# Strassen's seven products for 18 of the 22 gate/up pairs of each feed-forward, in a two-layer float32 decoder

## The chip, the cores and the metric

One NeuronCore of a Trainium2 chip runs the whole program. The metric is the device time of one execution in microseconds (us), as the median over runs. The engines are TensorE (PE; its weight loads are shown apart as PEld), VectorE (DVE), ScalarE (ACT), GpSimd (POOL), and SyncE (SP), whose queue issues most transfers.

## The reference

The input is one sequence of 512 tokens with 1024 features, in float32. Layer 0 is feed-forward, short gated convolution, feed-forward; layer 1 is feed-forward, differential attention over shared keys and values, feed-forward. Each of the four feed-forwards is

```
gate, up = jnp.split(x @ w_gu, 2, axis=-1)      # x: 512 x 1024, w_gu: 1024 x 5632
return (jax.nn.silu(gate) * up) @ w_down        # w_down: 2816 x 1024
```

with a norm before and after it. The change concerns the first product, `x @ w_gu`.

## The kernel before

Everything is kept as float32 and multiplied in three parts: a matrix is split into a rounded part `hi` (type fp32r) and the rest `lo`, and a product is hi·hi + hi·lo + lo·hi. The weights' `hi` is written by ACT (line 152) and `lo` by DVE (line 153); the activations `x_hi` and `x_lo` lie in SBUF transposed, features on the partitions, in 8 blocks of 128 features (`KT`) by 512 tokens.

The 2816 gate columns and 2816 up columns are handled as 22 pairs. A pair is one transfer of 1 MB (`raw`, two buffers) and two units: 1024 x 128 gate weights and 1024 x 128 up weights. For each unit `proj` runs 8 blocks x 3 parts = 24 matmuls of 512 tokens (line 169), into one of the two banks of a PSUM tile `gu`; ACT then takes silu of the gate (line 372), and DVE multiplies it by the up part into `praw` (line 374). The first three pairs of a feed-forward that follows another stage run in halves: first tokens 0 to 255, while the last tokens are still being normalized, then tokens 256 to 511 (`by_halves`). The feed-forward of layer 1 that follows the keys and values does not do so.

`down` then multiplies by `w_down` (line 220) in an order of its own (`two_then_two`), with `praw` split into `psp` just ahead. `WBUFS = 7` split units are held ahead of their use. PSUM holds three tiles `acc` of two banks and one tile `tp`, in which transposes are put. The order of instructions on each engine comes from a scheduler; each engine runs its queue in order.

Of the kernel before, what the change touches and what calls it, by code (L numbers as in the profile page):

```python
# [9 lines left out]
F32 = mybir.dt.float32  # L10
# [8 lines left out]
P = 128  # L19
# [11 lines left out]
WBUFS = 7  # L31
# [9 lines left out]
class Ahead:  # L41
# [21 lines left out]
    def done(self, i):  # L63
        self.closed.add(i)
        self.items[i] = None
        self.pump()

# [24 lines left out]
def trunk(ctx, tc, x, gu, dn, norm_g, cin, ck, cout, kvg, wk, wv, wq, lamp, subg, wo, out):  # L92
# [19 lines left out]

    def col_pairs(ap):
        return [ap[i].rearrange("p u k c -> p u (k c)") for i in range(ap.shape[0])]
# [5 lines left out]
    pairs, base = [], {}  # L120

    def stream(key, srcs):
        base[key] = 2 * len(pairs)
        pairs.extend(srcs)

    stream("gu00", col_pairs(gu[0, 0]))
    stream("dn00", row_pairs(dn[0, 0]))
    stream("cin", col_pairs(cin))
    stream("cout", row_pairs(cout))
    stream("gu01", col_pairs(gu[0, 1]))  # L130
    stream("dn01", row_pairs(dn[0, 1]))
    stream("k", col_pairs(wk))
    stream("v", row_pairs(wv))
    stream("gu10", col_pairs(gu[1, 0]))
    stream("dn10", row_pairs(dn[1, 0]))
    stream("q", col_pairs(wq))
    stream("wo", row_pairs(wo))
    stream("gu11", col_pairs(gu[1, 1]))
    stream("dn11", row_pairs(dn[1, 1]))
# [6 lines left out]
    raws = Ahead(load_pair, 2, len(pairs))  # L146

    def split_unit(i):
        raw = raws.get(i // 2)[:, i % 2, :]
        hi = wpool.tile([P, D], F32R, tag="whi", bufs=WBUFS, name="whi")  # L150
        lo = wpool.tile([P, D], F32R, tag="wlo", bufs=WBUFS, name="wlo")
        nc.scalar.activation(hi, raw, AF.Copy)  # L152
        nc.vector.tensor_tensor(lo, raw, hi.bitcast(F32), ALU.subtract)  # L153
        if i % 2:
            raws.done(i // 2)
        return hi, lo

    weights = Ahead(split_unit, WBUFS, 2 * len(pairs))


    def proj(o, key, u, xk, cols, ks=range(KT)):

        hi, lo = weights.get(base[key] + u)
        n = cols.stop - cols.start
        for k in ks:
            c = slice(k * P, (k + 1) * P)
# [6 lines left out]
    def close(key, u):  # L173
        weights.done(base[key] + u)
# [10 lines left out]
    def down(key, seq, parts, finish, tp_token=0, bufs=3):  # L185
# [22 lines left out]
        for n, (f, t) in enumerate(seq):  # L208
            if f is None:
                finish(t, y[t])  # L210
                continue
            if t not in y:
                if t >= 2:
                    later.keep(0)
                y[t] = tp_tile("y") if t == tp_token else acc_tile("y")
            hi, lo = weights.get(base[key] + f)
            ph, pl = ring.get(item_of[n])(t)
            for a, b in ((ph, hi), (ph, lo), (pl, hi)):
                for c in range(2):
                    nc.tensor.matmul(y[t][:, c, :], a, b[:, c * 512:(c + 1) * 512],  # L220
                                     start=(f == first[t] and a is ph and b is hi),
                                     stop=(f == last[t] and a is pl))
# [119 lines left out]
    def raw_parts(pool, praws):  # L342
        def parts(f, toks):
            a, n = toks[0] * P, len(toks) * P
            ps = pool.tile([P, 2, S], F32R, tag="psp", bufs=3, name="psp")
# [9 lines left out]
    def ffn(pool, l, i, xT, finish, halves=3):  # L355
# [5 lines left out]
        def job(f):  # L361
            def go(cols):
                if f not in tiles:
                    tiles[f] = acc_tile("gu")
                ps = tiles[f]
                for s in range(2):
                    proj(ps[:, s, :], "gu" + key, 2 * f + s, xk_of(xT), cols)
                    if cols.stop == S:
                        close("gu" + key, 2 * f + s)
                if cols.stop == S:  # L370
                    sil = pool.tile([P, S], F32, tag="sil", bufs=2, name="sil")
                    nc.scalar.activation(sil, ps[:, 0, :], AF.Silu)  # L372
                    praws[f] = place(f)
                    nc.vector.tensor_tensor(praws[f], sil, ps[:, 1, :], ALU.mult)  # L374
            return go

        by_halves([job(f) for f in range(NF)], halves)
# [5 lines left out]
    def conv(pool, xT, finish):  # L383
# [6 lines left out]
        def job_cz(ch):  # L390
            def go(cols):
# [7 lines left out]
                if cols.stop == S:  # L399
                    c = pool.tile([P, S], F32, tag="sil", bufs=2, name="c")  # L400
# [57 lines left out]
    def shared_kv(pool, xkv):  # L458
        tiles = {}

        def job(hd):
            def go(cols):
# [5 lines left out]
                if cols.stop == S:  # L468
                    close("k", hd)
                    kk = pool.tile([P, 2, S], F32R, tag="psp", bufs=3, name="kk")  # L470
# [14 lines left out]
        later.keep(0)  # L485

# [6 lines left out]
        def finish(t, y):  # L493
            for n in range(2):
                vs = pool.tile([P, S], F32, tag="sil", bufs=2, name="vs")
# [217 lines left out]
    with tc.tile_pool(name="big0", bufs=1, reuse_waits="tile") as pool:  # L713
# [4 lines left out]
        ffn(pool, 1, 0, holder["xT"], next_xT(norm_g[1, 2]), halves=0)  # L718
# [62 lines left out]
```

## Time and profile before

| | |
|---|---|
| median of 3 runs (range) | 1936.1 us (1936.01 to 1938.53) |
| the profiled execution | 1934.57 us |
| its span, first to last instruction | 1932.8 us |
| mean granted TensorE clock, as a share of full speed | 0.998 |
| busy: PE / DVE / ACT / POOL | 1897.1 / 752.3 / 616.9 / 99.6 us |
| read from HBM | 187.38 MB |

A busy PE is not necessarily a PE at its peak: a matmul's record is longer than the distance to the next one, since matmuls are pipelined. The distance between starts is therefore what a matmul costs. A row of idle time names what ended it.

### The profile page before, as it was taken

The numbers are of one execution on the slowest core, as the hardware profiler recorded it, in microseconds if no ns is written. First come the engines' busy times: TensorE is split into PE (matmuls) and PEld (weight loads), VectorE is DVE, ScalarE is ACT, GpSimd is POOL, SyncE is SP. The second block draws the span as 40 slices with busy tenths as digits, with TensorE's granted clock in tenths as the row PEclk, the third lists the DMA queues.
The fourth block names the chain that finished last, engine by engine and source line by source line (L and its number), as shares of the span: only waits on it lengthen the run. The fifth ranks groups of instructions, "written<-read, shape, count | busy, mean of one in ns | idle before, by whom it ended". The sixth has DMA issues, their size and how long they took to land. (4 is left out here: it accounts for less than half of the span.)

```text
span 1932.8 us, 22286 instructions
## 1 busy us (share of the span) xinstructions
PE 1897.1 (98%) x9376; PEld 1594.7 (83%) x9376; DVE 752.3 (39%) x978; ACT 616.9 (32%) x939; POOL 99.6 (5%) x234
## 2 busy tenths in 40 slices
PE   7999999999999999999999999999999999999998
PEld 7888888898889888888988888888886798888886
DVE  4322233554463222233633222233668463222333
ACT  4222222432243222223523222222457442222222
POOL 1000000000010000000200000000113210000000
PEclk9999999999999999999999999999999999999999
DMA  5332322232323232221354222222322033222221
GB/s 211 110 109 87 109 87 95 80 131 87 109 81 116 87 109 87 103 93 65 133 176 160 87 108 89 95 102 87 131 104 88 28 113 117 87 105 92 89 86 44
DMA packets 41508, 197.20 MB, mean 102 GB/s; under 512 B 3648, under 2 KB 8000, under 8 KB 27584
## 3 DMA queue, kind: packets, MB, share of 16 engines
q1 hardware_dynamic: 39616, 189.49, 27.6%
q0 software_dynamic: 1792, 6.29, 0.8%
q8 instruction: 73, 1.20, 0.2%
q14 instruction: 27, 0.22, 0.0%
HBM read 187.38 MB, written 8.39 MB: 101 GB/s over the span
## 5 line engine op out<-in xcount | busy, mean ns | idle before, releaser
L153 DVE TENSOR_TENSOR wlo<-raw,whi 128x1024 fp32r<-128x1024 f32 x328 | 401.1, 1224 | 770.0 <-ACT whi L152 769.6
L152 ACT ACTIVATE whi<-raw 128x1024 fp32r<-128x1024 f32 x328 | 346.3, 1057 | 833.1 <-PE gu L169 682.4
L169 PE MATMUL gu<-x_hi,whi 128*128 128x512 f32 (+1 forms) x1552 | 575.1, 371 | 1.3 <-ACT x_hi L297 1.3
L169 PE MATMUL gu<-x_lo,whi 128*128 128x512 f32 (+1 forms) x1552 | 574.6, 370 | 1.1 <-DVE x_lo L298 1.1
L169 PE MATMUL gu<-x_hi,wlo 128*128 128x512 f32 (+1 forms) x1552 | 574.4, 370 | 0.0
L220 PE MATMUL y<-whi,psp 128*128 128x512 f32 x1536 | 413.4, 390 | 0.0
L220 PEld LDWEIGHTS y<-whi,psp 128*128 128x128 f32 x1536 | 287.7, 188 | 59.3
L169 PEld LDWEIGHTS gu<-x_hi,whi 128*128 128x128 f32 x1552 | 293.8, 189 | 51.2 <-ACT x_hi L297 1.7
L169 PEld LDWEIGHTS gu<-x_lo,whi 128*128 128x128 f32 x1552 | 293.8, 189 | 50.1 <-DVE x_lo L298 1.4
L169 PEld LDWEIGHTS gu<-x_hi,wlo 128*128 128x128 f32 x1552 | 293.7, 189 | 49.5
L220 PE MATMUL y<-wlo,psp 128*128 128x512 f32 x768 | 236.6, 389 | 0.0
L220 PEld LDWEIGHTS y<-wlo,psp 128*128 128x128 f32 x768 | 144.2, 188 | 30.1
L298 DVE TENSOR_TENSOR psp<-praw,psp 128x512 fp32r<-128x512 f32 (+1 forms) x126 | 70.5, 563 | 250.3 <-ACT psp L297 250.3
L297 ACT ACTIVATE psp<-praw 128x512 fp32r<-128x512 f32 (+1 forms) x126 | 66.6, 528 | 317.5 <-PE y L220 309.0
L278 POOL TENSOR_SCALAR rb<-ss 128x1 f32<-128x1 f32 x84 | 27.1, 322 | 1737.7 <-ACT junk L275 1733.4
L374 DVE TENSOR_TENSOR praw<-sil,gu 128x512 f32<-128x512 f32 x88 | 59.8, 680 | 1.4 <-ACT sil L372 1.4
L169 PE MATMUL cz<-x_hi,whi 128*128 128x512 f32 (+1 forms) x160 | 55.6, 348 | 0.0
L169 PE MATMUL cz<-x_lo,whi 128*128 128x512 f32 (+1 forms) x160 | 55.4, 347 | 0.0
L169 PE MATMUL cz<-x_hi,wlo 128*128 128x512 f32 (+1 forms) x160 | 55.4, 347 | 0.0
L372 ACT ACTIVATE sil<-gu 128x512 f32<-128x512 f32 x88 | 50.8, 577 | 0.0
L308 DVE SCALAR_TENSOR_TENSOR xn<-h,rs,gpre 128x1024 f32<-128x1024 f32 x28 | 35.8, 1283 | 36.2 <-POOL rs L280 23.8
L280 POOL TENSOR_TENSOR rs<-rb,mhalf 128x1 f32<-128x1 f32 x84 | 49.2, 586 | 7.0
(105 smaller groups left out, 1313.6 us busy)
## 6 DMA issues: line engine op xcount, KB each, us to landing
raw<-gu SPq DMA_DIRECT2D x88, 1024.0 KB, 4.7
raw<-dn SPq DMA_DIRECT2D x44, 1024.0 KB, 4.7
raw<-cin SPq DMA_DIRECT2D x12, 1024.0 KB, 4.7
raw<-cout SPq DMA_DIRECT2D x4, 1024.0 KB, 4.8
raw<-wk SPq DMA_DIRECT2D x4, 1024.0 KB, 4.8
raw<-wv SPq DMA_DIRECT2D x4, 1024.0 KB, 5.4
kscr<-kk POOLq DMA_DIRECT2D x8, 512.0 KB, 6.3
raw<-wq SPq DMA_DIRECT2D x4, 1024.0 KB, 4.9
```

The costliest lines, as they stand in the source:

```text
L152: nc.scalar.activation(hi, raw, AF.Copy)
L153: nc.vector.tensor_tensor(lo, raw, hi.bitcast(F32), ALU.subtract)
L169: nc.tensor.matmul(o[:, cols], a[:, c], b[:, cols], start=(k == 0 and b is xh and a is hi), stop=(k == KT - 1 and a is lo))
L220: nc.tensor.matmul(y[t][:, c, :], a, b[:, c * 512:(c + 1) * 512], start=(f == first[t] and a is ph and b is hi), stop=(f == last[t] and a ...
L278: nc.gpsimd.tensor_scalar(b, ss, m / n, m * EPS, ALU.mult, ALU.add)
L280: nc.gpsimd.tensor_tensor(r, b, mhalf, ALU.pow)
L297: nc.scalar.activation(hi, src, AF.Copy)
L298: nc.vector.tensor_tensor(lo, src, hi.bitcast(F32), ALU.subtract)
L308: nc.vector.scalar_tensor_tensor(xn, h[t], r, g, ALU.mult, ALU.mult)
L372: nc.scalar.activation(sil, ps[:, 0, :], AF.Silu)
L374: nc.vector.tensor_tensor(praws[f], sil, ps[:, 1, :], ALU.mult)
```

## The change

Pairs 4 to 21 of each feed-forward (72 in all) are computed by one level of Strassen's algorithm in Winograd's form. The left matrix of a pair has four quarters of 512 features x 128 columns: `a11` and `a12` are the gate weights of the first and second 512 features, `a21` and `a22` the up weights. The right matrix has four quarters of 512 features x 256 tokens. Seven products of quarters (4 blocks x 3 parts = 12 matmuls of 256 tokens each) take the place of eight.

- Left factors (`Sum`): a11, a12, a22 as they are, and s1 = a21+a22, s2 = s1-a11, s3 = a11-a21, s4 = a12-s2. DVE forms the sums in PSUM (tile `sums`, in the place of `tp`), ACT writes `hi`, and `lo` comes from DVE for sums and from POOL for plain quarters.
- Right factors (`RightFactors`), once for each feed-forward: POOL puts x together again as `xr`, DVE forms t1 to t4; t1, t2, t3 take the place of three weight tiles `wt`, and t4 overwrites a quarter of `x_hi`/`x_lo`.
- The products go into three accumulators `a`, `b`, `c` (256 columns each; pairs take turns between the two banks). Between products, partial results are read out: u1 by ACT, u2, u3, g2 and both up halves `su` by DVE; POOL does the last multiplication into `praw`.
- Weights are held in 8 half tiles `wf` (512 features, hi and lo) and 3 whole tiles `wt`, together as much as the 7 units before. Units of the other stages use both kinds by turns; in a half tile a unit takes two ACT and two DVE instructions.

```diff
+            plain = {"a11": a11, "a12": a12, "a22": a22}.get(self.form)
+            if plain is not None:
+                nc.scalar.activation(hi, plain, AF.Copy)
+                nc.gpsimd.tensor_tensor(lo, plain, hi.bitcast(F32), ALU.subtract)
+                Sum.flush()
+            else:
+                if self.form == "s2":
+                    Sum.psum = tp_tile("sums")
+                s0, s1 = Sum.psum[:, 0, :], Sum.psum[:, 1, :]
+                if self.form == "s2":
+                    nc.vector.tensor_tensor(s0, a21, a22, ALU.add)
+                    nc.vector.tensor_tensor(s1, s0, a11, ALU.subtract)
+                    src = s1
+                elif self.form == "s1":
+                    src = s0
+                elif self.form == "s3":
+                    Sum.flush()
+                    nc.vector.tensor_tensor(s0, a11, a21, ALU.subtract)
+                    src = s0
+                else:
+                    Sum.flush()
+                    nc.vector.tensor_tensor(s1, a12, s1, ALU.subtract)
+                    src = s1
+                nc.scalar.activation(hi, src, AF.Copy)
+                Sum.flush()
+                Sum.pending.append((self, lambda: nc.vector.tensor_tensor(lo, src, hi.bitcast(F32), ALU.subtract)))
...
+    FORMS = ("a11", "s2", "s1", "s3", "a12", "s4", "a22")
...
+            self.x = pool.tile([P, KT, S], F32, tag="praw", bufs=3, name="xr")
+            for k in range(0, KT, 2):
+                nc.gpsimd.tensor_tensor(self.x[:, k:k + 2, :], self.hi[:, k:k + 2, :].bitcast(F32),
+                                        self.lo[:, k:k + 2, :].bitcast(F32), ALU.add)
...
+            def after6():
+                nc.vector.tensor_tensor(u2, b, u1, ALU.add)
+
+            def after7():
+                nc.vector.tensor_tensor(u3, b, u1, ALU.add)
+                nc.vector.tensor_tensor(su[:, 1, RIGHT], c, u3, ALU.add)
+
+            def after3():
+                nc.vector.tensor_tensor(g2, c, u2, ALU.add)
+                nc.scalar.activation(su[:, 0, RIGHT], g2, AF.Silu)
+
+            def after4():
+                nc.vector.tensor_tensor(su[:, 1, LEFT], b, u1, ALU.add)
+                praws[f] = place(f)
+                nc.gpsimd.tensor_tensor(praws[f], su[:, 0, :], su[:, 1, :], ALU.mult)
+
+            step(a, "a11", "b11", True, True, lambda: nc.scalar.activation(u1, a, AF.Copy))
+            step(b, "s2", "t2", True, True, after6)
+            step(c, "s1", "t1", True, True, lambda: None)
+            step(b, "s3", "t3", False, True, after7)
+            step(a, "a12", "b21", False, True, lambda: nc.scalar.activation(su[:, 0, LEFT], a, AF.Silu))
+            step(c, "s4", "b22", False, True, after3)
+            step(b, "a22", "t4", False, True, after4)
...
+        right.four()
+        for f in range(PLAIN, NF):
+            seven(f, (f - PLAIN) % 2)
```

**DVE, in the middle of a feed-forward's gate/up stage.** Before, a pair has two `lo` parts of weights and the multiplication by silu (the numbers tell tiles apart):

```order
L153 TENSOR_TENSOR wlo_4396<-raw_4307,whi_4395 128x1024
L374 TENSOR_TENSOR praw_4092<-sil_4399,gu_4340 128x512
L153 TENSOR_TENSOR wlo_4428<-raw_4307,whi_4427 128x1024
L153 TENSOR_TENSOR wlo_4458<-raw_4369,whi_4457 128x1024
L374 TENSOR_TENSOR praw_4092<-sil_4461,gu_4402 128x512
```

Now a pair has thirteen, in this order: L598 is u2, L229 the `lo` of a sum, L221 the sum s3, L601 is u3, L602 the right half of `su` (it reads `c`), L225 the sum s4, L605 g2, L214 and L215 the sums s1 and s2 of a later pair, L609 the left half of `su`. The tile `u_775` belongs to the pair that PE multiplies; `sums_791` are the factors of the next pair, `sums_917` those of the one after it:

```order
L598 TENSOR_TENSOR u_775<-b_650,u_775 128x256
L229 TENSOR_TENSOR wf_790<-sums_791,wf_790 128x512
L229 TENSOR_TENSOR wf_808<-sums_791,wf_808 128x512
L221 TENSOR_TENSOR sums_791<-raw_639 128x512
L601 TENSOR_TENSOR u_775<-b_650,u_775 128x256
L229 TENSOR_TENSOR wf_823<-sums_791,wf_823 128x512
L602 TENSOR_TENSOR su_776<-c_651,u_775 128x256
L225 TENSOR_TENSOR sums_791<-raw_639,sums_791 128x512
L229 TENSOR_TENSOR wf_858<-sums_791,wf_858 128x512
L605 TENSOR_TENSOR u_775<-c_651,u_775 128x256
L214 TENSOR_TENSOR sums_917<-raw_756 128x512
L609 TENSOR_TENSOR su_776<-b_650,u_775 128x256
```

Between u3 (L601) and the right half of `su` (L602), which frees `c`, the `lo` part of s3 (L229) has been put; the sum for a later pair (L214) stands ahead of the left half of `su` (L609), which frees `b`.

**PE, at the same place.** Before, units follow each other in groups of three matmuls (here the last group of the gate and the first of the up unit):

```order
L169 MATMUL gu_934<-x_hi_96,whi_740 128x512
L169 MATMUL gu_934<-x_lo_97,whi_740 128x512
L169 MATMUL gu_934<-x_hi_96,wlo_741 128x512
L169 MATMUL gu_934<-x_hi_96,whi_772 128x512
L169 MATMUL gu_934<-x_lo_97,whi_772 128x512
L169 MATMUL gu_934<-x_hi_96,wlo_773 128x512
```

Now, from the end of the product with a12 (`wf_1090`) to the product with s4 (`wf_1107`); `wf_1124` is a22:

```order
L336 MATMUL a_1147<-x_lo_97,wf_1090 128x256
L336 MATMUL a_1147<-x_hi_96,wf_1090 128x256 x2
L336 MATMUL a_1147<-x_lo_97,wf_1090 128x256
L336 MATMUL a_1147<-x_hi_96,wf_1090 128x256
L336 MATMUL b_1148<-x_hi_96,wf_1124 128x256
L336 MATMUL b_1148<-x_lo_97,wf_1124 128x256
L336 MATMUL c_1149<-x_hi_96,wf_1107 128x256
L336 MATMUL c_1149<-x_lo_97,wf_1107 128x256
L336 MATMUL c_1149<-x_hi_96,wf_1107 128x256 x2
```

Two of the twelve matmuls of the product with a22 have been moved ahead of the product with s4; the other ten follow it. This is so in 17 of the 18 pairs of a feed-forward; in the last one they stand in the order of the code.

**POOL, at the same place.** Before, POOL has no instruction there. Now it has four for each pair, three `lo` parts of plain quarters (L207: a12 and a22 of the next pair, a11 of the one after) and the multiplication into `praw` (L611):

```order
L207 TENSOR_TENSOR wf_841<-raw_639,wf_841 128x512
L207 TENSOR_TENSOR wf_875<-raw_639,wf_875 128x512
L207 TENSOR_TENSOR wf_895<-raw_756,wf_895 128x512
L611 TENSOR_TENSOR praw_445<-su_776 128x512
L207 TENSOR_TENSOR wf_967<-raw_756,wf_967 128x512
```

The multiplication of a pair stands behind three splits, of which the third is for a pair two places on.

## Rows read from the trace of the kernel before

**Rows 1.** The page: busy us (share of the span) and instructions; granted clock in tenths.

```profile
PE 1897.1 (98%) x9376; PEld 1594.7 (83%) x9376; DVE 752.3 (39%) x978; ACT 616.9 (32%) x939; POOL 99.6 (5%) x234
...
PEclk9999999999999999999999999999999999999999
```

**Rows 2.** Groups by line and form: count | busy us, mean ns | idle before, releaser.

```profile
L169 PE MATMUL gu<-x_hi,whi 128*128 128x512 f32 x1264 | 491.7, 389 | 0.0
...
L153 DVE TENSOR_TENSOR wlo<-raw,whi 128x1024 fp32r<-128x1024 f32 x328 | 401.1, 1224 | 770.0 <-ACT whi L152 769.6
L152 ACT ACTIVATE whi<-raw 128x1024 fp32r<-128x1024 f32 x328 | 346.3, 1057 | 833.1 <-PE gu L169 682.4 <-PE cz L169 57.6 <-PE b L169 28.4
```

**Rows 3.** Waits of PE: us in total, times, longest.

```profile
PE xps L313 <- DVE xn L308: 12.8, 6, 9.8
...
PE gu L169 <- ACT x_hi L297: 1.3, 1, 1.3
```

**Rows 4.** PE in order of time, 256 tokens wide, first feed-forward: start us, us.

```profile
40.00 0.28 PE L169 MATMUL gu<-x_hi,wlo 128*128 128x256 f32 x1
...
42.88 0.28 PE L169 MATMUL gu<-x_hi,wlo 128*128 128x256 f32 x1
```

**Rows 5.** PE in order of time, 512 tokens wide, first feed-forward.

```profile
101.50 0.39 PE L169 MATMUL gu<-x_hi,whi 128*128 128x512 f32 x1
...
104.22 0.39 PE L169 MATMUL gu<-x_hi,whi 128*128 128x512 f32 x1
```

**Rows 6.** Groups by line and form, DVE and ACT, smaller tiles.

```profile
L298 DVE TENSOR_TENSOR psp<-praw,psp 128x512 fp32r<-128x512 f32 x66 | 45.7, 692 | 174.5 <-ACT psp L297 174.5
L298 DVE TENSOR_TENSOR psp<-praw,psp 128x256 fp32r<-128x256 f32 x60 | 24.9, 421 | 75.7 <-ACT psp L297 75.7
...
L297 ACT ACTIVATE x_hi<-att_ps 128x512 fp32r<-128x512 f32 x8 | 4.7, 593 | 7.3 <-PE att_ps L633 6.4 <-DVE m L574 0.9
```

**Rows 7.** DVE in order of time, two like instructions back to back, merged (two stretches).

```profile
366.25 0.75 DVE L298 TENSOR_TENSOR psp<-praw,psp 128x256 fp32r<-128x256 f32 x2
...
962.92 1.28 DVE L298 TENSOR_TENSOR kk<-kps,kk 128x512 fp32r<-128x512 f32 x2
```

**Rows 8.** In order of time: PE's last matmul into b, and DVE's reading of b.

```profile
437.32 0.39 PE L169 MATMUL b<-x_hi,wlo 128*128 128x512 f32 x1
...
437.75 0.69 DVE L420 TENSOR_TENSOR praw<-praw,b 128x512 f32<-128x512 f32 x1 [0.61 <-PE b L169]
```

**Rows 9.** In order of time: DVE frees a PSUM bank, and PE goes on.

```profile
970.71 0.69 DVE L298 TENSOR_TENSOR kk<-kps,kk 128x512 fp32r<-128x512 f32 x1 [0.32 <-ACT kk L297]
...
971.45 0.50 PE L169 MATMUL kps<-xkv,whi 128*128 128x256 f32 x2 [0.25 <-DVE kk L298]
...
971.79 0.28 PE L169 MATMUL kps<-xkv,wlo 128*128 128x256 f32 x1
...
971.91 0.40 PE L169 MATMUL kps<-xkv,whi 128*128 128x256 f32 x2
```

**Rows 10.** Instructions of one tile, POOL: count, duration ns min/median/max.

```profile
L537 POOL TENSOR_SCALAR bias<-dist x8: 613/617/922, 1388.4 to 1490.1; 128x512 f32<-128x512 f32 x8
...
L617 POOL TENSOR_TENSOR rr<-rs,r x32: 189/190/729, 1431.1 to 1523.6; 128x1 f32<-128x1 f32 x32
```

**Rows 11.** In order of time: a small POOL instruction under DVE's xn.

```profile
936.04 0.55 POOL L280 TENSOR_TENSOR rs<-rb,mhalf 128x1 f32<-128x1 f32 x1
...
936.62 1.28 DVE L308 SCALAR_TENSOR_TENSOR xn<-h,rs,gpre 128x1024 f32<-128x1024 f32 x1 [0.71 <-POOL rs L280]
...
936.84 1.48 POOL L280 TENSOR_TENSOR rs<-rb,mhalf 128x1 f32<-128x1 f32 x1
```

**Rows 12.** In order of time: POOL beside a DVE instruction that reads PSUM.

```profile
1388.39 1.20 POOL L537 TENSOR_SCALAR bias<-dist 128x512 f32<-128x512 f32 x2
1388.45 1.28 DVE L287 SCALAR_TENSOR_TENSOR tmp<-y,rs,gpost 128x1024 f32<-128x1024 f32 x1 [0.97 <-POOL rs L280]
```

**Rows 13.** Transfers: queue, count, KB each, us from issue to landing.

```profile
raw<-gu SPq DMA_DIRECT2D x88, 1024.0 KB, 4.7
```

More of the change, by code (lines that the diff above doesn't have):

```diff
@@ L66, in done, with __init__, free, take @@
         self.pump()
+class Slots:
+    def __init__(self, cap):
+        self.cap, self.given = cap, []
+    def free(self, n):
+        i = len(self.given) - self.cap
+        return all(self.given[j] for j in range(max(i, 0), max(i + n, 0)))
+    def take(self):
+        self.given.append(False)
+        return len(self.given) - 1
+    def give(self, i):
+        self.given[i] = True
 class Later:
@@ L144, in load_pair @@
         return raw
[L146 to L158, printed above, removed]
+    raws = Ahead(load_pair, 2)
@@ new lines, in trunk, with __init__, free, make @@
+    class Sum:
+        pending = []
+        psum = None
+        def __init__(self, pair, form):
+            self.pair, self.form = pair, form
+        def free(self):
+            return half_slots.free(1)
+        def make(self):
+            raw = raws.get(self.pair)
+            a11, a12, a21, a22 = (raw[:, u, h * 512:(h + 1) * 512] for u in range(2) for h in range(2))
+            w, slot = half_tile()
+            hi, lo = w[:, 0, :], w[:, 1, :]
+            self.halves, self.slots = [(hi, lo)], [slot]
+            plain = {"a11": a11, "a12": a12, "a22": a22}.get(self.form)
[17 more added lines that the diff above has]
+                    src = s0
+                else:
+                    Sum.flush()
[4 more added lines that the diff above has]
+                Sum.pending.append((self, lambda: nc.vector.tensor_tensor(lo, src, hi.bitcast(F32), ALU.subtract)))
+            if self.form == FORMS[-1]:
+                raws.done(self.pair)
+        @staticmethod
+        def flush():
+            while Sum.pending:
+                Sum.pending.pop(0)[1]()
+        def ready(self):
+            if any(e is self for e, _ in Sum.pending):
+                Sum.flush()
@@ new lines, in trunk, with add_units, add_sums @@
+    FORMS = ("a11", "s2", "s1", "s3", "a12", "s4", "a22")
+    def add_units(key, srcs, kind):
+        for j, src in enumerate(srcs):
+            pairs.append(src)
+            for u in range(2):
+                index[key, 2 * j + u] = len(entries)
+                entries.append(Unit(len(pairs) - 1, u, kind(2 * j + u)))
+    def add_sums(key, f, src):
+        pairs.append(src)
+        for form in FORMS:
+            index[key, f, form] = len(entries)
+            entries.append(Sum(len(pairs) - 1, form))
@@ L171, in proj, with close, product @@
             later.tick(3 * 0.21 * n / 512)
-    def close(key, u):
-        weights.done(base[key] + u)
+    def close(*key):
+        weights.done(*key)
+    def product(o, key, xk, first, last):
+        hi, lo = weights.get(*key)[0]
+        for k in range(4):
+            c = slice(k * P, (k + 1) * P)
+            xh, xl = xk(k)
+            for a, b in ((hi, xh), (hi, xl), (lo, xh)):
+                nc.tensor.matmul(o, a[:, c], b, start=(first and k == 0 and b is xh and a is hi),
+                                 stop=(last and k == 3 and a is lo), skip_group_check=True)
+            later.tick(3 * 0.21 * 256 / 512)
     def two_then_two(nf, tail, stag):
@@ new lines, in seven, with step @@
+        def seven(f, e):
+            if e == 0:
+                tiles["abc"] = [acc_tile(n) for n in "abc"]
+            a, b, c = (t[:, e, LEFT] for t in tiles["abc"])
+            tmp = work.tile([P, 4, 256], F32, tag="tmp", bufs=2, name="u")
+            u1, u2, u3, g2 = (tmp[:, n, :] for n in range(4))
+            su = pool.tile([P, 2, S], F32, tag="pair", bufs=3, name="su")
+            def step(o, form, factor, first, last, then):
+                product(o, ("gu" + key, f, form), right.t[factor], first, last)
+                then()
+                if f == NF - 1 and factor in right.slots:
+                    right.done(factor)
+                close("gu" + key, f, form)
+            def after6():
[8 more added lines that the diff above has]
+                nc.vector.tensor_tensor(su[:, 1, LEFT], b, u1, ALU.add)
+                praws[f] = place(f)
+                nc.gpsimd.tensor_tensor(praws[f], su[:, 0, :], su[:, 1, :], ALU.mult)
[6 more added lines that the diff above has]
+            step(b, "a22", "t4", False, True, after4)
@@ L378, in ffn @@
+        if halves:
+            later.keep(2)
+            for f in range(3):
+                job(f, FIRST)
+            later.keep(0)
+            right = RightFactors(pool, xT)
+        for f in range(PLAIN):
+            job(f, SECOND if halves and f < 3 else ALL)
+            if f == 1:
+                right.one_three()
+            if f == 2:
+                right.two()
+        right.four()
+        for f in range(PLAIN, NF):
+            seven(f, (f - PLAIN) % 2)
         g_post = bcast(norm_g[l, 1 if i == 0 else 5], "gpost")
```

175 lines of the change are left out of this document (129 added, 46 removed).

## The prediction

> **What bounds the kernel now.** I read the page of the profile first, then the groups by line and form, the waits of PE, and short stretches in order of time. PE is busy 98% of the span at a granted clock of 0.998 of full speed, the upper of its two levels (2.4 GHz) [rows 1]. Its longest wait totals 12.8 us, and on this stage's matmuls it waits 1.3 us once, at the start [rows 3]. So the kernel is as long as its matmuls, and a matmul costs the distance to the next start. 512 tokens wide, twelve steps take 104.22 - 101.50 = 2.72 us, 0.2267 us each, though the record says 0.39 [rows 5]. 256 wide, 24 steps take 42.88 - 40.00 = 2.88 us, 0.120 us each [rows 4]. Half the width is thus more than half the price: 0.2267 = 2 x 0.1067 + 0.0133, a fixed 0.013 us for each matmul.
>
> DVE and ACT wait for PE here: ACT's splits of weights spent 682.4 us waiting for PE to free a tile, and DVE's waited for ACT's [rows 2]. They have room; the question is whether they have enough, and in time.
>
> **PE's work.** A pair had 2 units x 24 = 48 matmuls of 512 tokens: 48 x 0.2267 = 10.88 us. It gets 7 x 12 = 84 of 256: 84 x 0.120 = 10.08 us. That is 0.80 us less, 7.4% instead of the 12.5% that seven for eight suggests, because 84 fixed parts replace 48. For 18 x 4 = 72 pairs: **-57.6 us**. Weights loaded afresh for every matmul are in the 0.120 already, since the row's kernel loads them so too.
>
> The Trainium skill, "TensorE: Matmul & The Clock Gate", section "Wait — 56ns, not 53.3ns?", gives for another number type a spacing of columns / 2.4 GHz + 2.5 ns; an estimate by it is 84 x 0.109 against 48 x 0.216 us, 1.19 us a pair, -86 us in all. The rows show a fixed part five times as large, so I go by them.
>
> **Load of the other engines in a pair.** Two DVE instructions of 512 elements back to back start 1.28 - 0.68 = 0.60 us apart, two of 256 start 0.75 - 0.42 = 0.33 us apart, each ending about 0.09 later than its successor starts [rows 6, 7]. DVE gets 4 sums and 4 lo parts of 512, and 5 results of 256: 8 x 0.60 + 5 x 0.33 = 6.5 us of 10.08. ACT gets 7 hi parts and three of 256: 7 x 0.59 + 3 x 0.42 = 5.4 us at most, the 0.42 taken from DVE [rows 6]. No row has DVE writing float32 sums to PSUM; the bounds are 0.60 us (as in every row) and 1.2 us (write as dear as read). I take 0.60, since reading PSUM makes no difference either (kk, psp).
>
> POOL gets four two-input instructions of 512 elements; no row has one. With one input 512 elements took 617 ns, and a two-input one of a single element 190 ns [rows 10], so an element costs about (617 - 190) / 512, 0.43 us for 512. Low bound 0.62 us (the second input free), high 0.19 + 4 x 0.43 = 1.9 us (four passes); I take two passes, 0.19 + 0.86 = 1.05 us, 4.2 us a pair.
> The Trainium skill, "GPSIMD Engine Reference", section 3.1, has 4497 ns for 2048 elements, from which 1.1 to 1.3 us is an estimate here.
>
> **The chain that matters.** `b` and `c` are read between two products that write them. Take the pair's first matmul as 0: products start at 0 (a11), 1.44 (s2), 2.88 (s1), 4.32 (s3), 5.76 (a12), and end at 10.08. Of a22, two matmuls run at 7.20, ahead of s4, which starts at 7.44. A reader starts 0.04 us after the record of the last matmul ends [rows 8]; the 256-wide record is 0.28 long [rows 4], so 0.20 us after the next start. PE goes on 0.05 us after DVE's record ends (970.71 + 0.69 to 971.45), and its second matmul then starts 0.22 instead of 0.12 later: 0.10 for the restart [rows 9].
>
> - u2 at 2.88 + 0.20 = 3.08; lo(s2) and lo(s1) from 3.41 to 4.61; then the sum s3, which waits for the end of lo(s1), from 4.7 to 5.4; ACT's hi(s3) to 6.05.
> - s3's product ends at 5.76, so u3 starts at 5.96, lo(s3) at 6.29 (hi is 0.24 early), the half of su that reads c at 6.89. It ends at 7.31; PE may write c at 7.36.
> - s4's product is due at 7.44. **0.08 us to spare**, less than the restart's 0.10. I charge 0.02 us a pair: 1.4 us.
>
> In the last pair of each feed-forward the two matmuls were not moved; there s4 is due at 7.20 and loses 0.16 + 0.10 us: 4 x 0.26 = 1.0 us. Behind this wait stands everything on PE, and a delay moves the whole pair. The others have more room: u2 frees b at about 3.55 for 4.32; the left su frees b at 10.08 + 0.20 + 0.42 + 0.05 = 10.75 for 11.52; u1 is needed 2.9 us after ACT can do it.
>
> **Once in each feed-forward.** POOL's four sums of 1024 elements for `xr` take about 4 x 1.9 = 7.6 us, and the t factors cost DVE 8 x 1.13 = 9 us and ACT 4 us. In three feed-forwards they lie under the second halves of pairs 0 to 2 and under pair 3 (3 x 24 x 2 x 0.120 + 10.88 = 28 us), in the other under 43 us of whole pairs. I charge 0; without the cover it would be up to 9 us each. Splitting a unit by halves costs two fixed parts (0.07 us each on DVE) in engines that wait; the ring still holds seven units' worth, and where it is refilled late, at a stage's end, the first units are split 2 us before their use. `raw` is loaded in 4.7 us [rows 13], as often as before, one in 10 us. At the kernel's start the first unit's second part may add 0.1 us.
>
> **Sum.** -57.6 + 1.4 + 1.0 + 0.1 = -55.1. The profiled execution took 1934.57 us (span 1932.8), 1.5 under the median: 1934.57 - 55.1 = 1879.5, span 1877.7, and for the median 1936.1 - 55.1 = **1881 us**. What a measurement can tell from no change is about 0.2%, 4 us.
>
> **Rivals.**
>
> *c comes late* (0.22). 0.08 us is little: dearer PSUM writes put hi(s3) behind u3 (a sum of 1.2 us ends at 5.9, hi at 6.6, su at 7.6, 0.2 late, with restart 0.3), and so does any wait of DVE between u3 and su. Against it: every duration is from a row of the same shape. 0.1 to 0.4 us a pair: 1888 to 1910 us.
>
> *POOL gets in ahead of the sum s1* (0.08). An instruction of DVE with two SBUF inputs and one of POOL shut each other out: under `xn` POOL's took 1.48 us instead of 0.55 and ended 0.42 after xn [rows 11], while beside `tmp`, whose large input is PSUM, POOL ran its usual 0.6 [rows 12]. That DVE waits in its turn, no row shows. Of a pair's DVE instructions only two sums have two SBUF inputs, s1 and s3. DVE reaches s1 of a later pair at about 9.5, POOL its split of a22 at 9.76. Were POOL first, s1 would start at 10.8, the left su at 11.4, and b be free at 11.87 instead of by 11.52; 0.35 + 0.10 us, in every second pair (the other takes another bank): 36 x 0.45 = +16, 1897 us.
> The Trainium skill, "SBUF — State Buffer", section "Who interferes with whom", states this as a rule: the shared port is a lock that goes to whoever starts first. By that rule the order at 9.5 decides, and the trace agrees for POOL's side (1.48 us).
>
> *POOL holds up s3: slower* (0.05). POOL's queue for a pair runs from the end of s1's sum, 10.2, through two splits and the multiplication, to 10.2 + 3P, which is 0.12 + 3P in the next pair, where DVE wants the sum s3 at 4.7. s3 can be 0.24 + 0.08 late; so from P = 1.63 us the chain slips, and with the restart's 0.10 a pair loses the 0.80 that it gained from P = 1.9. At 1.9, the high bound, it is 5.82 - 5.02 + 0.10 = 0.9 us, 72 x 0.9 = 65 us: 1944 us. Against it: it takes nearly twice the 1.05 that I work out.
>
> *A smaller fixed part* (0.02). If the new matmuls paid a fifth of the 0.0133 us, a pair would take 84 x (0.1067 + 0.0027) = 9.2 us, 1.7 less: 72 x 1.7 = 122, 1817 us with the same losses. Against it: the run of 256 wide matmuls, in the same three-part sequence, paid it in full [rows 4].
> This is what the spacing in "TensorE: Matmul & The Clock Gate" (the Trainium skill, the section named above) would make of the new matmuls; the rows disagree with it, at 0.120 us.
>
> *Setting up the factors shows* (0.05): up to 9 us in each feed-forward, 1881 + 36 = 1917 us.
>
> **How the numbers follow.** The forecast's case, 1877 to 1886, has 0.58. The range, 1875 to 1906, takes in most of the late c and POOL ahead of s1, about 0.85 in all. Faster by over 0.2%: 0.94; slower: 0.05, the case of POOL; within 0.2%: 0.01.
>
> **What would show it.** Right: 84 matmuls a pair 0.120 apart, pairs 10.1 us apart, PE waiting for L602 by at most some hundredths, POOL's 512 near 1.05 us, its splits of a22 behind the sum s1. Wrong: idle time of PE before c's matmuls that DVE ends, each pair (the chain); before b's in every second pair (POOL first); POOL above 1.6 us; a gap before pair 4 (factors).

## The result, and the profile after

In one comparison the changed kernel took 1909.2 us (median of 4 runs, 1908.2 to 1910.8) and the kernel before 1937.3 us: a ratio of 0.9855, 95% interval 0.9838 to 0.9872. It is faster, by half of what was forecast: 1881 us was predicted, 1906 was the upper end of the range, and the time lies 3 us above it. The profiled span fell from 1932.8 to 1907.8 us, by 25.0. The sums below go by these two profiles; by the medians the gain is 28.1 us, because the profiled run of before (1934.57 us) was faster than all four of this comparison and that of the changed kernel (1910.82 us) the slowest of its four.

The page of the kernel after (busy us, share, instructions; then groups), to be read beside [rows 1] and [rows 2]:

```profile
PE 1861.6 (98%) x11968; PEld 1677.9 (88%) x11968; DVE 1109.1 (58%) x1837; ACT 828.9 (43%) x1566; POOL 528.2 (28%) x538
...
PEclk9999999999999999999999999999999999999999
...
L207 POOL TENSOR_TENSOR wf<-raw,wf 128x512 fp32r<-128x512 f32 x216 | 294.2, 1374 | 440.3 <-ACT wf L206 440.3
```

PE is still busy for 98% of the span at the same clock, so the share says nothing of what went wrong. The two views that do are the stretches of the 18 Strassen pairs of each feed-forward (start:end, length, busy time of the product's line) and the waits (us in total, times, longest). First the stretches, from the first a11 matmul to the first matmul of the down product:

```profile
65.43:253.23 187.80, 185.71 (x1512) 182.22 (x1511) 1.00 0.31 107
607.12:794.72 187.60, 185.71 (x1512) 182.22 (x1511) 1.00 0.32 107
1059.36:1246.98 187.62, 185.72 (x1512) 182.22 (x1511) 1.00 0.32 107
1591.81:1779.41 187.60, 185.71 (x1512) 182.21 (x1511) 1.00 0.32 107
sum 750.62, PE 742.86 PEld 728.87; mean PE 185.71 PEld 182.22
```

1512 matmuls are 18 x 84, all of them. 72 pairs at 10.08 us would be 725.8 us; they took 750.6, or 10.42 us a pair. **24.9 us are lost here.** The other (57.6 - 24.9) - 25.0 = 7.7 us are lost elsewhere; by the medians it would be 4.6. The waits of the kernel after, to be read beside [rows 3]:

```profile
PEld c L336 <- DVE su L602: 21.6, 68, 0.7
...
DVE wf L229 <- POOL praw L611: 17.8, 63, 0.6
...
PE xps L477 <- DVE xn L472: 15.7, 10, 9.1
```

The weights of the matmuls that write `c` wait for line 602, the half of `su` that reads `c`: 68 times, in every pair but the last of each feed-forward. That is the rival *c comes late*. One pair in order of time, of which the first matmul stood at 127.95 (its a12 product, 5.76 later, starts at 133.71; L206 is ACT's `hi` of a plain quarter, here a12 of the next pair):

```profile
130.47 1.31 POOL L611 TENSOR_TENSOR praw<-su 128x512 f32<-128x512 f32 x1
...
131.09 0.60 ACT L227 ACTIVATE wf<-sums 128x512 fp32r<-128x512 f32 x1 [0.57 <-PE b L336]
131.10 0.42 DVE L598 TENSOR_TENSOR u<-b,u 128x256 f32<-128x256 f32 x1 [1.92 <-PE b L336]
131.79 1.29 DVE L229 TENSOR_TENSOR wf<-sums,wf 128x512 fp32r<-128x512 f32 x2 [0.26 <-POOL praw L611]
...
133.11 0.70 DVE L221 TENSOR_TENSOR sums<-raw 128x512 f32<-128x512 f32 x1
...
133.91 0.42 DVE L601 TENSOR_TENSOR u<-b,u 128x256 f32<-128x256 f32 x1
133.93 0.60 ACT L227 ACTIVATE wf<-sums 128x512 fp32r<-128x512 f32 x1 [2.24 <-PE b L336]
...
134.42 0.62 ACT L206 ACTIVATE wf<-raw 128x512 fp32r<-128x512 f32 x1
...
134.56 0.69 DVE L229 TENSOR_TENSOR wf<-sums,wf 128x512 fp32r<-128x512 f32 x1 [0.23 <-ACT wf L227]
...
135.17 0.41 DVE L602 TENSOR_TENSOR su<-c,u 128x256 f32<-128x256 f32 x1
135.27 0.28 PE L336 MATMUL b<-x_lo,wf 128*128 128x256 f32 x1
...
135.64 0.39 PE L336 MATMUL c<-x_hi,wf 128*128 128x256 f32 x1
135.86 0.28 PE L336 MATMUL c<-x_lo,wf 128*128 128x256 f32 x1
...
137.85 0.69 DVE L214 TENSOR_TENSOR sums<-raw 128x512 f32<-128x512 f32 x1
...
138.14 1.55 POOL L207 TENSOR_TENSOR wf<-raw,wf 128x512 fp32r<-128x512 f32 x1 [1.73 <-ACT wf L206]
```

`u2` (line 598) starts at 3.15 of the pair, where 3.08 was forecast. Then lo(s2) (line 229, the first of two) should follow 0.33 us behind; it follows after 0.69, at 3.84. Of the 0.43 us against the forecast's 3.41, `u2` brings 0.07 and the wait 0.36. What follows is late: the sum s3 at 5.16, hi(s3) from 5.98 to 6.58 instead of until 6.05, `u3` on time at 5.96, lo(s3) at 6.61, and `su` from 7.22 to 7.64. `c` was due 0.12 after b's second matmul, at 135.39 (7.44 of the pair); it starts at 135.64, 0.25 late, and its second matmul comes 0.22 instead of 0.12 later. That is 0.35 us in this pair; the 24.9 us over the 68 pairs that stop are 0.37 each.

The row of hi(s3) names PE's product with s3 as its releaser. That can't be: in the code the `hi` of the next pair's s3 is written when the product with s1 has released its half tile, ahead of the product with s3. It follows the sum s3 by 0.12 us here, and by 0.11 in the next kernel below, where the row names the sum.

What held lo(s2)? ACT's hi(s1) runs until 131.69, and POOL's multiplication until 131.78; DVE starts at 131.79. (hi(s1) itself starts no earlier because, by the ring of eight half tiles, it is written into the tile that the product with s2 has just released: its row names PE's `b`, as that of `u2` does.) The row of lo(s2) names POOL. Two theories: **ACT** (lo(s2) waits for hi(s1), though it doesn't use it: both read the tile `sums`) and **POOL** (its multiplication holds DVE). Before them stands the reckoning of the prediction, that it waits for neither.

### The profile page after: what moved, and what is told of

Read it like the earlier page. It is cut to its first block, busy times and chain, and to the rows that moved or that the text cites. A ratio compares the mean times of both kernels' runs of the same rounds, so it can differ in the third digit from the quotient of the medians.

```text
span 1907.8 us, 29851 instructions
## 1 busy us (share of the span) xinstructions
PE 1861.6 (98%) x11968; PEld 1677.9 (88%) x11968; DVE 1109.1 (58%) x1837; ACT 828.9 (43%) x1566; POOL 528.2 (28%) x538
## 5 line engine op out<-in xcount | busy, mean ns | idle before, releaser
L207 POOL TENSOR_TENSOR wf<-raw,wf 128x512 fp32r<-128x512 f32 x216 | 294.2, 1374 | 440.3 <-ACT wf L206 440.3
L384 PE MATMUL y<-wf,psp 128*128 128x512 f32 x1344 | 310.2, 389 | 0.0
L384 PEld LDWEIGHTS y<-wf,psp 128*128 128x128 f32 x1344 | 251.8, 188 | 51.9
L229 DVE TENSOR_TENSOR wf<-sums,wf 128x512 fp32r<-128x512 f32 x288 | 192.4, 689 | 100.5 <-ACT wf L227 82.4
L178 ACT ACTIVATE wf<-raw 128x512 fp32r<-128x512 f32 x214 | 131.1, 626 | 243.3 <-PE y L384 126.2
L336 PE MATMUL b<-wt,wf 128*128 128x256 f32 x1728 | 230.8, 283 | 0.0
L336 PE MATMUL a<-x_hi,wf 128*128 128x256 f32 x1152 | 230.8, 283 | 0.0
L384 PE MATMUL y<-wt,psp 128*128 128x512 f32 x960 | 222.6, 389 | 0.0
L336 PEld LDWEIGHTS b<-wt,wf 128*128 128x128 f32 x1728 | 217.7, 192 | 0.0
L336 PEld LDWEIGHTS a<-x_hi,wf 128*128 128x128 f32 x1152 | 190.1, 192 | 0.2
L206 ACT ACTIVATE wf<-raw 128x512 fp32r<-128x512 f32 x216 | 136.1, 630 | 69.0 <-PE c L336 37.7
```

Of the source, the lines that this page charges most:

```text
L178: nc.scalar.activation(hi, raw[:, a * 512:(a + 1) * 512], AF.Copy)
L206: nc.scalar.activation(hi, plain, AF.Copy)
L207: nc.gpsimd.tensor_tensor(lo, plain, hi.bitcast(F32), ALU.subtract)
L229: Sum.pending.append((self, lambda: nc.vector.tensor_tensor(lo, src, hi.bitcast(F32), ALU.subtract)))
L336: nc.tensor.matmul(o, a[:, c], b, start=(first and k == 0 and b is xh and a is hi), stop=(last and k == 3 and a is lo), skip_group_check=True)
L384: nc.tensor.matmul(y[t][:, c, :], a, w[c][b], start=(f == first[t] and a is ph and b == 0), stop=(f == last[t] and a is pl))
```

## The experiments

### c read first

```
+def after1():                                            # behind the product s1
+    nc.vector.tensor_tensor(u3, c, u1, ALU.add)
 def after7():
-    nc.vector.tensor_tensor(u3, b, u1, ALU.add)
-    nc.vector.tensor_tensor(su[:, 1, RIGHT], c, u3, ALU.add)
+    nc.vector.tensor_tensor(su[:, 1, RIGHT], b, u3, ALU.add)
 ...
-step(c, "s1", "t1", True, True, lambda: None)
+step(c, "s1", "t1", True, True, after1)
```

> The half of su that needs c is built the other way round: v = c + u1 as soon as s1's product is in c, then su = b + v after s3's product. As many DVE instructions of the same size; c is read 1.4 us before its next product is due, b as early as before. Both theories (the first lo part waits for ACT's hi(s1), or for POOL's multiplication) put the loss on c being read too late, so both expect the 0.25 us stall and the 0.09 us restart to vanish: pairs 10.08 us apart instead of 10.42, 72 x 0.342 = 24.6 us less, 1885 us (1882 to 1889). If pairs stay above 10.3 us apart, c's reader is not what PE waits for.

It took 1895.3 us (ratio to before 0.9791, 0.9777 to 0.9806), 10 us over what both theories gave. No matmul waits for `c` any more: all steps to it are 0.120 us. The edit also changed PE's order: the two matmuls of a22 now stand behind the product with s4 in all 72 pairs (below, b's first at 135.12 follows c's last), so `c` was due at 7.20 of the pair and not at 7.44, and was still in time. It is so in the next kernel too, and in those with POOL's split behind s1 and c read first. But another wait stands in its place, as the waits of this kernel show:

```profile
PE b L336 <- DVE su L611: 5.3, 32, 0.4
```

32 of the 72 pairs now stop before b's first product. In order of time:

```profile
135.00 0.28 PE L336 MATMUL c<-x_hi,wf 128*128 128x256 f32 x1
135.12 0.28 PE L336 MATMUL b<-x_hi,wf 128*128 128x256 f32 x1
...
136.09 2.98 POOL L207 TENSOR_TENSOR wf<-raw,wf 128x512 fp32r<-128x512 f32 x2 [0.95 <-ACT wf L206]
...
136.38 1.56 DVE L214 TENSOR_TENSOR sums<-raw 128x512 f32<-128x512 f32 x1
...
137.86 0.41 DVE L611 TENSOR_TENSOR su<-b,u 128x256 f32<-128x256 f32 x1
137.88 0.28 PE L336 MATMUL a<-x_hi,wf 128*128 128x256 f32 x1
...
138.32 0.39 PE L336 MATMUL b<-wt,wf 128*128 128x256 f32 x1 [0.16 <-DVE su L611]
```

The sum s1 (line 214, both inputs in SBUF) takes 1.56 us instead of 0.69. POOL's split of a22 began 0.29 us before it and takes 1.29 (two in a row, 2.98); DVE's record ends 0.56 after that. The left half of `su` is pushed behind, and b is 0.32 us late (138.32 instead of 138.00), in every second pair. This is the second rival, *POOL gets in ahead of the sum s1*. In the changed kernel it is the other way round, by 0.3 us: s1 began first and took 0.69, and POOL's split took 1.55 (the last two rows of the pair shown above).

The stretches of 18 pairs are 184.8 us here, in sum 739.1: 13.4 us over 725.8, of which 32 x 0.32 are the stall and the rest the restart.

### su ahead of lo(s3)

```
-nc.vector.tensor_tensor(su[:, 1, RIGHT], c, u3, ALU.add)
+Sum.after = nc.vector.tensor_tensor(su[:, 1, RIGHT], c, u3, ALU.add).ins
 ...
 i = nc.vector.tensor_tensor(lo, src, hi.bitcast(F32), ALU.subtract)
+if self.form == "s3" and Sum.after is not None:
+    tc.add_manual_dep(i.ins, Sum.after.name, ..., reason="order")    # order only, no wait
```

> One order edge: lo(s3) may not be issued before the half of su that reads c. Then su starts behind u3, at about 6.4 us of the pair instead of 7.2, and c is free near 6.9, 0.5 us before it is due at 7.44. If lo(s3) between u3 and su makes the loss: no stall, pairs 10.08 apart, 1885 us (1882 to 1889). If DVE is late because it has too much work in a pair, lo(s3) moved back only shifts the wait to b or to a product of the next pair, and 1900 to 1909 us is kept.

1896.0 us (0.9796, 0.9780 to 0.9813): the same result by another way. `su` started 0.46 us behind `u3`, no step to `c` was longer than 0.120 us, and the same 32 pairs stopped before b, with the same sum s1 of 1.56 us; the stretches sum to 738.9 us. The time lies between the two alternatives. The first was right about `c`; the second was right that the wait moves to b, but not about the cause: it is not the amount of DVE's work, as POOL's split behind the sum s1 shows below.

### lo(s2) ahead of hi(s1)

```
 elif self.form == "s1":
+    Sum.flush()                       # writes lo(s2) here, ahead of hi(s1)
     src = s0
```

(and order edges that keep u3, lo(s3), su as they were)

> lo(s2) is written ahead of hi(s1) instead of behind it; the rest of DVE's order stays (u2, lo(s2), lo(s1), sum s3, u3, lo(s3), su). Theory ACT (the two wait for each other because both read the tile that holds the sums, whichever is written first): lo(s2) starts 0.33 us after u2 instead of 0.69, but hi(s1) then starts only behind lo(s2); lo(s1), s3, hi(s3), lo(s3) and su come some 0.4 us later than now, the stall grows from 0.25 to about 0.7: pairs near 10.85 us apart, about 1940 us. Theory POOL: lo(s2) still starts when POOL's multiplication ends, 0.69 us after u2. The reckoning of the prediction (no wait between the two): no stall, 1885 us.

1910.7 us in one run, where theory ACT gave 1940, and the prediction's reckoning 1885. The mechanism is that of theory ACT, as DVE and ACT show in order of time:

```profile
128.01 1.68 DVE L220 TENSOR_TENSOR sums<-raw 128x512 f32<-128x512 f32 x1
...
130.52 0.60 ACT L234 ACTIVATE wf<-sums 128x512 fp32r<-128x512 f32 x1 [0.97 <-DVE sums L221]
130.62 0.42 DVE L614 TENSOR_TENSOR u<-b,u 128x256 f32<-128x256 f32 x1 [0.19 <-PE b L352]
...
131.15 0.69 DVE L238 TENSOR_TENSOR wf<-sums,wf 128x512 fp32r<-128x512 f32 x1
131.93 0.60 ACT L234 ACTIVATE wf<-sums 128x512 fp32r<-128x512 f32 x1 [0.82 <-DVE wf L238]
132.56 0.69 DVE L238 TENSOR_TENSOR wf<-sums,wf 128x512 fp32r<-128x512 f32 x1 [0.72 <-ACT wf L234]
```

hi(s1) now starts 0.09 us behind the end of lo(s2), which it doesn't use, and 1.3 us after `u2` began instead of beside it. The two have only the tile `sums` in common, and the one that is written later waits for the other. That it is not the order of writing alone, the changed kernel shows: there lo(s3) is written behind ACT's `hi` of a12, which doesn't read `sums`, and starts at 134.56, 0.03 us after its own hi(s3) and under that of a12 (134.42, 0.62 long). lo(s2) itself came 0.53 us after `u2` here, not 0.33: the sum s1 was held up by POOL (1.68 us), so that hi(s2), which lo(s2) does use, ran until 131.12. `su` started 7.88 us into the pair, 0.66 later than in the changed kernel. The time was missed mainly for a reason that has nothing to do with the wait: the scheduler moved seven matmuls of a22 ahead of s4 instead of two, so that `c` was due at 8.04 instead of 7.44, and the stall grew from 0.25 to 0.30 us only. Part of the 0.66 comes from the late s1 and not from the order of lo(s2) and hi(s1); the run doesn't part the two.

### POOL's multiplication left out

```
-nc.gpsimd.tensor_tensor(praws[f], su[:, 0, :], su[:, 1, :], ALU.mult)
+nc.gpsimd.tensor_copy(praws[f], su[:, 0, :])
```

> POOL's last instruction of a pair copies silu(gate) instead of multiplying it by the up half (that multiplication is left out): one input instead of two, about 0.62 instead of 1.31 us, so POOL is done 0.7 us earlier. Theory ACT: lo(s2) still starts 0.69 us after u2, pairs stay 10.42 us apart, 1909 us (1906 to 1911). Theory POOL: lo(s2) starts 0.33 us after u2 and the stall in front of c goes, 1885 us.

1909.4 us in one run: theory POOL falls. A pair in order of time:

```profile
77.38 0.60 POOL L611 COPY praw<-su 128x512 f32<-128x512 f32 x1
...
77.95 1.28 POOL L207 TENSOR_TENSOR wf<-raw,wf 128x512 fp32r<-128x512 f32 x1
...
79.28 0.42 DVE L598 TENSOR_TENSOR u<-b,u 128x256 f32<-128x256 f32 x1 [1.92 <-PE b L336]
79.97 0.69 DVE L229 TENSOR_TENSOR wf<-sums,wf 128x512 fp32r<-128x512 f32 x1 [0.27 <-ACT wf L227]
```

POOL is done at 79.23, before `u2` starts, and lo(s2) still comes 0.69 us after `u2`. The releaser named in the changed kernel's row was a coincidence: POOL's end and ACT's end lay 0.09 us apart. In this kernel the row names ACT.

### POOL's split behind the sum s1

```
 if self.form == "a22":
-    nc.gpsimd.tensor_tensor(lo, plain, hi.bitcast(F32), ALU.subtract)
+    Sum.late.append((self, low))      # the same instruction, written later:
 ...
-nc.vector.tensor_tensor(s0, a21, a22, ALU.add)
+Sum.go(nc.vector.tensor_tensor(s0, a21, a22, ALU.add))   # waits for this sum
```

> c_read_first, and POOL's split of a22 waits for the end of the next pair's sum s1 (it is used 9 us later). In c_read_first the stall moved to b in 32 of 72 pairs, 0.32 us + restart, and sum s1 took 1.56 us instead of 0.69 where POOL's split had begun 0.29 us before it. Theory shared port (who begins first holds the other up): s1 back at 0.69 us, no stall in front of b, pairs 10.08 us apart, 32 x 0.41 = 13 us less than c_read_first: 1882 us (1880 to 1885). Rival, DVE has too much work in a pair: s1 is short again but b or c still comes late, 1890 us or more.

1883.2 us (0.9716, 0.9701 to 0.9731). Both stalls are gone; the pair that corresponds, in order of time, and the sum of the four stretches:

```profile
136.42 0.69 DVE L230 TENSOR_TENSOR sums<-raw 128x512 f32<-128x512 f32 x1
...
137.02 0.42 DVE L627 TENSOR_TENSOR su<-b,u 128x256 f32<-128x256 f32 x1
137.25 1.29 POOL L219 TENSOR_TENSOR wf<-raw,wf 128x512 fp32r<-128x512 f32 x1 [2.07 <-DVE sums L230]
```

```profile
sum 725.74, PE 725.73 PEld 725.53; mean PE 181.43 PEld 181.38
```

s1 takes 0.69 us, POOL's split 1.29, and a pair 725.7 / 72 = 10.08 us: the predicted number, with PE busy without a break.

### The same without reading c first

The last edit, in the changed kernel alone.

> The changed kernel with POOL's split of a22 behind sum s1, and c read as late as in the changed kernel. There the late c sets the pair and sum s1 is not held up, so taking POOL away gives nothing: pairs 10.42 us apart, 1909 us (1906 to 1911). If POOL costs something in the changed kernel itself: 1896 to 1903 us.

1908.1 us in one run, stretches of 750.6 us in sum, as without it. POOL's split ahead of s1 costs nothing as long as `c` comes late, and 13.4 us in the pairs (11.0 of the span) with `c` read first.

### The rings alone

Of the 7.7 us lost outside the pairs, the waits show a part: PE's waits for the norm's `xn` in front of the transposes are 12.8 us in [rows 3] with a longest, at the kernel's start, of 9.8, so 3.0 elsewhere, and in the kernel after 15.7 with 9.1, so 6.6. That is 3.6 us more, and another 0.9 for `tmp` (2.6 against 1.7); the rest was not traced to a wait.

```
-PLAIN = 4
+PLAIN = NF                                  # no Strassen
-entries.append(Unit(len(pairs) - 1, u, kind(2 * j + u)))
+entries.append(Unit(len(pairs) - 1, u, len(entries) % 7 >= 4))
```

> No Strassen: all 22 pairs of each feed-forward by 48 matmuls of 512 tokens, but the weights in the changed kernel's rings (8 half units and 3 whole ones; 4 units in 7 are split by halves). Theory rings (the 6.8 us that are lost at the five stage changes, where the last token's transposes come late, are due to the splits by halves standing ahead of that token's norm on ACT and DVE): 5 to 8 us over the kernel before, 1941 to 1944 us. If they are due to Strassen's own factors and sums: 1936 us, as before.

1953.9 us (1.0076, 1.0057 to 1.0094): outside both expectations, and no evidence for the one it seems to favour. PE's waits for `xn` are 12.4 us with a longest of 10.0, as small as before. Of the 20.3 us by which the span grew, the waits show 12.5 us in other places: at the start of the down products, where `psp` and `sil` now share three buffers,

```profile
PE y L384 <- ACT psp L461: 7.7, 4, 2.1
```

(3.2 us more of the same for DVE's part of `psp`), and in attention (`att_ps` for `q`, 3.1 us against 1.5). The rest was not traced. What it did show is that splits by halves as such don't make the norms late. Here which units are whole follows another count.

### The norms ahead

```
+with tc.high_priority(offset=200):
     post_norm(t, y, g_post, half)
     pre_norm(t, targets, ...)
```

(on top of c read first)

> c_read_first, and the norms between two stages get a higher priority with the scheduler, which then lets one split by halves instead of three stand between the norm's instructions of the last token at most places, and four at one. Theory rings: 1 to 4 us less than c_read_first, 1891 to 1894 us, with the last transposes of a stage change less late. If the splits don't matter: 1895 us.

1901.3 us (0.9807, 0.9793 to 0.9822), not faster than c read first: the profiled spans are 1897.3 and 1893.4. PE's waits for `xn` fell from 15.7 to 14.5 us, but those of the transposes for `x_lo`, which frees their tile, rose from 1.9 to 4.3 (longest 2.4 instead of 0.7). `x_lo` is written outside the part with the higher priority. So what one DVE instruction gained, the next one lost, and more. The time lies above both expectations, these waits account for 1.2 of the 3.9 us by which the span grew, and the test doesn't tell the two expectations apart.

### Which units are whole

Units are split in a fixed order, and a whole unit needs a whole slot. In the changed kernel the last whole units of a down product are in use until its last token, so that the next stage's first whole units, and all behind them, are split under the last token's norm. On DVE, at the first stage change of the kernel after:

```profile
379.95 1.28 DVE L472 SCALAR_TENSOR_TENSOR xn<-h,rs,gpre 128x1024 f32<-128x1024 f32 x1 [0.85 <-POOL rs L444]
381.15 1.89 DVE L180 TENSOR_TENSOR wf<-raw,wf 128x512 fp32r<-128x512 f32 x3
382.96 1.28 DVE L451 SCALAR_TENSOR_TENSOR tmp<-y,rs,gpost 128x1024 f32<-128x1024 f32 x1
...
387.75 1.28 DVE L472 SCALAR_TENSOR_TENSOR xn<-h,rs,gpre 128x1024 f32<-128x1024 f32 x1
```

Three splits stand between the third token's `xn` and the last one's `tmp`.

```
-add_units("dn00", row_pairs(dn[0, 0]), turns(0))                # and dn01, dn10, dn11
-add_units("cout", row_pairs(cout), turns(3 + 24))
-add_units("wo", row_pairs(wo), turns(3 + KT))
+add_units("dn00", row_pairs(dn[0, 0]), turns(2))
+add_units("cout", row_pairs(cout), turns(2))
+add_units("wo", row_pairs(wo), turns(2))
```

On top of POOL's split behind s1:

> pool_later with another choice of which units are split whole: in the stages that end with norms (the down products, cout, wo) the last three units, which are in use up to the last token, are now units by halves, so that the whole slots are free early and fewer splits wait, in their fixed order, for the stage's last matmul. Theory: splitting stands in order, and behind a whole unit whose slot is freed last some five units must be split under the last token's norm, where the kernel before had three; then the transposes of the last token come as in the kernel before (0 to 0.2 us late at the first, third and fourth stage change instead of 1.13, 0.2 at the second instead of 1.70, 1.9 at the last instead of 2.72): 5 to 6.5 us less than pool_later, 1877 us (1876 to 1879). If the splits by halves themselves are too dear: 1882 to 1884 us, gaps as now.

1878.9 us (0.9698, 0.9683 to 0.9713), **the best kernel here**. Its span is 1877.1 us against 1882.4, 5.3 less, the lower end of what was expected; by the medians, which come from two comparisons, it is 4.3 less. The same place:

```profile
373.57 1.30 DVE L488 SCALAR_TENSOR_TENSOR xn<-h,rs,gpre 128x1024 f32<-128x1024 f32 x1 [0.72 <-POOL rs L460]
374.80 0.68 DVE L181 TENSOR_TENSOR wf<-raw,wf 128x512 fp32r<-128x512 f32 x1
...
375.40 1.27 DVE L467 SCALAR_TENSOR_TENSOR tmp<-y,rs,gpost 128x1024 f32<-128x1024 f32 x1
...
380.14 1.28 DVE L488 SCALAR_TENSOR_TENSOR xn<-h,rs,gpre 128x1024 f32<-128x1024 f32 x1 [1.07 <-POOL rs L460]
```

and the waits of the kernel as a whole:

```profile
PE xps L493 <- DVE xn L488: 12.8, 8, 9.4
```

One split stands there now, the last token's `xn` follows the third's by 6.57 us instead of 7.80, and the waits for `xn` outside the start are 3.4 us, near the 3.0 of the kernel before.

And in the changed kernel alone:

> The same choice of whole units in the changed kernel itself, nothing else changed: pairs stay 10.42 us apart; 5 to 6.5 us less than the changed kernel's 1909, 1903 us (1902 to 1905). If the splits by halves themselves are too dear: 1908 to 1910 us.

1905.7 us (0.9838, 0.9819 to 0.9856), just above the expected range; the span is 1903.9, 3.9 less than the changed kernel's 1907.8. The pairs did not stay as they were: the four stretches sum to 753.4 us, 2.8 more. Outside them it gained 6.7 us, slightly more than expected.

## Why the prediction was wrong

**The gain of PE's work: right.** The kernel with both waits removed runs its 72 pairs in 725.7 us, 10.08 us each, with every matmul 0.120 us from the next. In the kernel before, the same pairs take 195.84 us in each feed-forward, 783.4 in all, so -57.6 us is what it had to be. By the spacing in "TensorE: Matmul & The Clock Gate" (the Trainium skill, the section "Wait — 56ns, not 53.3ns?") an estimate would have been 0.109 us a matmul; these runs disagree with it, as the rows of before did.

**The step that failed** is "lo(s2) and lo(s1) from 3.41 to 4.61" in the chain. It took both to be free once DVE was, and looked for a wait on ACT only at lo(s3). lo(s2) waits for ACT's hi(s1), and that runs beside `u2`, which ends before it: lo(s2) came at 3.84. The slip of 0.43 us (0.36 of it the wait) was 0.53 at the end of hi(s3), 0.33 at `su` (hi(s3) had a margin of 0.24) and 0.25 at `c`, after the 0.08 to spare; with the restart 0.35 us in that pair. The +1.4 us of the sum, charged for this wait at s4's product, was 24.9. That `c` is read too late is shown by c read first and by su ahead of lo(s3), which both remove the stop; that lo(s2) waits for hi(s1) and not for POOL is shown by POOL's copy and by lo(s2) ahead of hi(s1). Two things are argued and not shown: that the wait comes from the shared tile `sums`, from the two having nothing else in common (two tiles for the sums were not tried, since PSUM is full), and that without it `su` would have been in time, from the chain's own times. No run takes this wait away and leaves the rest.

**The rival was right in its place and price** (0.1 to 0.4 us a pair, 1888 to 1910 us), and wrong in the cause that it named first, dearer PSUM writes: DVE's writes to PSUM took 0.69 to 0.70 us, as its other instructions of 512 elements that nothing held up. Its second, "any wait of DVE between u3 and su", did occur, 0.23 us for hi(s3), but as the consequence of the wait at lo(s2), three DVE instructions ahead of `u3`, which it didn't name.

**POOL ahead of the sum s1** was given as a rival at 36 x 0.45 us. It cost 13.4 us in 32 pairs, 0.42 each, but not in the changed kernel. Each rival was priced as if only one could happen. Here the first hid the second. DVE reaches s1 at 9.90 us of the pair in the changed kernel and with c read first (whose pair began at 126.48) alike; POOL's split, which waits for ACT's `hi` of a22 and so for the end of s4's product, comes at 10.19 in the one and at 9.61 in the other. Of these 0.58 us, 0.35 are the stop at `c` that is gone, and 0.24 the two matmuls that no longer stand ahead of s4.
The Trainium skill, "SBUF — State Buffer", section "Who interferes with whom", has it that a DVE instruction with two SBUF inputs contends with a POOL instruction that reads SBUF, and that who issues first has the shared pair for the whole instruction. The traces agree, now from DVE's side too: 1.56 us instead of 0.69 behind POOL, and with the order changed 0.69 again.

**POOL holds up s3** did not happen: its two-input instruction of 512 elements took 1.29 us alone, against 1.05 assumed and 1.63 needed. The estimate of 1.1 to 1.3 us from "GPSIMD Engine Reference" of the Trainium skill, section 3.1, was the better one.

**The last pair of each feed-forward** was charged 1.0 us and cost nothing: it has no next pair whose sums would stand on DVE, and the step to `c` is 0.120 us there. **Setting up the factors** costs nothing, as charged: no wait of PE for a right factor stands in the waits, and there is no gap ahead of pair 4.

**Outside the pairs** 0.1 us was charged and 7.7 lost (4.6 by the medians). The text said that "where it is refilled late, at a stage's end, the first units are split 2 us before their use", and took that for harmless, since PE does not wait for the units. It waits for the norm that shares DVE with them. Another choice of whole units gave 5.3 us back. With all three edits the span is 55.7 us under that of before, and the median 57.8 us under that of its own comparison; the forecast's sum was 55.1. That it comes so near is no merit of the forecast, which was for the kernel without these edits.

## What to carry to other kernels

When a chain has less to spare than one instruction, list for each instruction on it what the program makes it wait for, not only what it uses: two engines that read different banks of one tile waited for each other here. A stall that a rival predicts may be hidden by an earlier one; after removing a wait, look for the next and don't book its whole price as gain. A row's releaser is the one that ended last, and with two candidates 0.09 us apart only an experiment that moves one of them tells them apart.

## What the runs showed of the hardware that had not been expected

- Some instructions of DVE and ACT that wait for more than one semaphore are preceded by a separate semaphore instruction (in the changed kernel's trace 68 of the 72 `u2` are, and no `u3`). In the pair above hi(s1) and `u2` started 0.10 and 0.11 us after the record of s2's last matmul ended (130.71 + 0.28), where `u3`, without that extra instruction, started 0.04 us after s3's (133.59 + 0.28). Such a wait made the start later by 0.06 to 0.07 us.
- POOL with two SBUF inputs took 1.29 us for 512 elements, and 1.55 when DVE's two-input sum began 0.3 us before it; with one input it took 0.60. DVE's sum took 0.69 us, and 1.56 when POOL's split began 0.29 us before it.
- A wait of 0.25 us before one matmul costs 0.35: the next two starts are 0.22 apart instead of 0.12, as in [rows 9].
